# Grouping a chunked scan's 64-column matmuls by two chunks, with the steps around them moved

## The chip, the cores and the metric

The kernel runs on one core of a Trainium2 chip. The metric is the time of the whole program on the device in microseconds (us), the median of several runs. The core has a matrix engine (TensorE, PE in the profile, with PEld for its weight loads), a vector engine (VectorE, DVE), an activation engine (ScalarE, ACT), a general engine (GpSimd, POOL) and SyncE (SP), which here only issues DMAs. Each engine works through its own instructions in a fixed order and waits for the others by semaphores.

## The reference

Two layers over a sequence of 1024 positions with 1024 features: first a gated MLP that mixes positions inside chunks, then a Mamba-2 mixer. The change touches the second one only:

```python
xbc = silu(causal_depthwise_conv(xbc, conv_w, conv_b))      # x, B, C
dt  = softplus(dt_raw + dt_bias);  A = -exp(a_log)
dA_cs = cumsum(dt * A)                                      # inside each chunk of 128 positions
decay = exp(where(causal, dA_cs[l] - dA_cs[s], -inf))
w_ls  = (C @ B.T) * decay * dt                              # 128 x 128 per chunk and head
y_diag = w_ls @ x
states = (B * exp(dA_cs[-1] - dA_cs) * dt).T @ x            # per chunk
prev[c + 1] = prev[c] * exp(dA_cs[-1]) + states[c]          # over the chunks
y_off  = (C @ prev) * exp(dA_cs)
y = y_diag + y_off + x * d_skip
gated = rmsnorm(y * silu(z)) over each group of 256 features
h = h + gated @ w_out
```

There are 8 groups of 4 heads with 64 features each, a state of 128 per group, and 8 chunks of 128 positions.

## The kernel before, in words

The part in question is `scans()`. It goes through 64 steps `n`, one for each pair of group `g` and chunk `c` (chunk innermost), and writes the instructions of every engine in that order by hand (`tc.manual_schedule()`); each engine then executes its own list in order. For one chunk there are these pieces:

- `load`: a DMA brings the cumulated decays of the chunk's 4 heads to a tile `wl` (128x512; 4 such buffers). `decay`: ACT turns it into exponentials (L1582 four times, then L1584).
- `pe_a`: PE transposes x (two tiles) and B (L1576) and multiplies C by B (L1577) into one PSUM tile `tp`.
- `tokens`: DVE scales x out of `tp` (L1590) and masks the C·B product (L1592), ACT copies B (L1594), POOL scales x once more (L1595). Together they fill the tile `cw`.
- `weights`: DVE multiplies the exponentials by the masked product (L1600), so `wl` now holds w_ls.
- `pe_b`: PE's part that needs all this. Four matmuls with 64-column weights give y_diag (L1609: head pairs write to the lower and upper 64 partitions of `yy`), two give y_off from the state of the chunk before (L1613), one gives this chunk's own state (L1620, `sp`).
- `carry` (POOL, L1630) and `update` (DVE, L1639, or L1637 for the first chunk) step the state on.
- `out`: DVE multiplies y_off by its decay (L1651), adds the skip path to y_diag (L1654 twice), and POOL adds the two (L1657). `gate`: POOL multiplies by silu(z) (L1661).
- Every fourth chunk, the sums of squares for the group norm: `squares` (ACT, L1672), `sum_a` (POOL, L1679), `sum_b` (PE: matmuls with one column of ones, L1685, into the free half of `sp`; then two ACT copies of one row each, L1689), `sum_c` (a DMA). `group_rstd` reads these back and makes the reciprocal root (DVE L1704, L150 to L153).

In between, `project(upto)` emits background matmuls, six per step of its counter (L134 to L136, 128x512 each, one float32 product split in three): the input projections of later groups up to step 50, output-projection products after that. Behind each 48 of them stands an accumulator `ab` that has to pass the convolution: ACT starts it (L1311), DVE adds three taps (L1305), and after two accumulators ACT applies silu (L1416, which loads another activation table first; the next exponential loads the old table again). These conv pieces sit in a list `queue`; `drain()` emits one per chunk, and the beginning of the next accumulator emits what is still left of the older ones. Preparing the projections' weights takes a cast on ACT (L111) and a subtraction of 128x1024 on DVE or, in the scan, on POOL (L112).

For chunk n the order in the loop is: `pe_b(n)`, half of the background matmuls, `pe_a(n+2)`, `weights(n+1)`, `update(n)`, `out(n)`, `decay(n+2)`, `carry(n+1)`, `drain()`, `tokens(n+2)`, `gate(n)`, `load(n+3)`, the pieces of the norm, the other half of the background.

Of the kernel before, what the change touches and what calls it, by code (L numbers as in the profile page):

```python
# [11 lines left out]
ALU = mybir.AluOpType  # L12
# [3 lines left out]
P = 128  # L16
# [6 lines left out]
G = 8  # L23
# [6 lines left out]
def kernel(  # L30
# [21 lines left out]
    nc = tc.nc  # L52
    x = x[0]
    out = out[0]
# [19 lines left out]
    def k1(shape, name):  # L74
        return sb.tile(shape, F32, name=name, tag="k1", bufs=3)
# [21 lines left out]
    def sm(name):  # L97
        return ps[0].tile([P, 512], F32, name=name, tag="sm", bufs=n_sm[0])
# [65 lines left out]
    ones = cst.tile([P, P], F32, name="ones")  # L164
# [387 lines left out]
    for gp in range(G // 2):  # L552
# [4 lines left out]
        if gp == 1:  # L557
# [9 lines left out]
            for h in range(2):  # L567
# [9 lines left out]
                for k in range(4):  # L577
                    g = h * 4 + k
# [648 lines left out]
    V = nc.vector  # L1227
# [319 lines left out]
    class Scan:  # L1547


        def __init__(self, g, eng):  # L1550
            self.g, self.st, self.eng = g, sts[g], eng
            self.wl, self.tp, self.cw, self.ps, self.state = {}, {}, {}, {}, {}
            if g < G - 1:
                gd.append(dr.tile([P, 2, T], F32, name=f"g_d{g}"))
            else:
                gd.append(self.st["x"])
# [43 lines left out]
            V.tensor_tensor(out=wl, in0=wl, in1=self.cw[c][:, 640:768].unsqueeze(1).broadcast_to([P, 4, P]),  # L1600
                            op=ALU.mult)

        def pe_b(self, c, ends=None):

            w, wl = self.cw[c], self.wl.pop(c)
            yy = sm("yy")
            for j in range(4):
                pt, f = j // 2, j % 2
                nc.tensor.matmul(out=yy[f * 64:(f + 1) * 64, pt * P:(pt + 1) * P], lhsT=w[:, j * 64:(j + 1) * 64],  # L1609
                                 rhs=wl[:, j, :], start=True, stop=True)  # L1610
            if c > 0:
                for pt in range(2):
                    nc.tensor.matmul(out=yy[:, 256 + pt * P:384 + pt * P],  # L1613
                                     lhsT=self.state[c - 1][:, pt * P:(pt + 1) * P], rhs=self.x(3, c),
                                     start=True, stop=True)
            sp = None
            if c < 7 or ends is not None:
                sp = sm("sp")
            if c < 7:
                nc.tensor.matmul(out=sp[:, 0:256], lhsT=w[:, 512:640], rhs=w[:, 256:512], start=True, stop=True)  # L1620
            if ends is not None:
                ends.sum_b(sp[:, 256:512], 2 if ends.g == G - 1 else 1)
            self.ps[c] = yy, sp

        def carry(self, c):

# [7 lines left out]
        def update(self, c):  # L1634
            if c == 0:
                self.state[0] = k1([P, 256], "state")
                V.tensor_copy(out=self.state[0], in_=self.ps[0][1][:, 0:256])  # L1637
            elif c < 7:
                V.tensor_tensor(out=self.state[c], in0=self.ps[c][1][:, 0:256], in1=self.state[c], op=ALU.add)  # L1639

        def y(self, c):

# [1 line left out]
                return self.z(c)  # L1644
            return self.cw[c][:, 768:1024].rearrange("p (m l) -> p m l", m=2)

        def out(self, c):
            yy, t2 = self.ps.pop(c)[0], self.y(c)
            if c > 0:
                t1 = k1([P, 2, P], "t1")  # L1650
                V.tensor_tensor(out=t1, in0=yy[:, 256:512].rearrange("p (m l) -> p m l", m=2),  # L1651
                                in1=self.st["ze", c // 4][:, 2:4, c % 4 * P:c % 4 * P + P], op=ALU.mult)
            for pt in range(2):
                V.scalar_tensor_tensor(t2[:, pt, :], self.x(pt, c), dsk[:, 2 * self.g + pt:2 * self.g + pt + 1],  # L1654
                                       yy[:, pt * P:(pt + 1) * P], ALU.mult, ALU.add)
            if c > 0:
                self.eng.tensor_tensor(out=t2, in0=t2, in1=t1, op=ALU.add)  # L1657

        def gate(self, c):
# [21 lines left out]
        def sum_b(self, pr=None, n=1):  # L1681
            pr = sm("pr") if pr is None else pr
            for m in range(n):
                for h in range(2):
                    nc.tensor.matmul(out=pr[h * 64:h * 64 + 1, 0:256], lhsT=ones[:, 0:1],  # L1685
                                     rhs=self.sq[:, m, h * 256:(h + 1) * 256], start=m == 0, stop=m == n - 1)
            self.sr = self.sq[:, 1, 0:256]
            for h in range(2):
                nc.scalar.copy(out=self.sr[h * 64:h * 64 + 1], in_=pr[h * 64:h * 64 + 1, 0:256])  # L1689
# [143 lines left out]
    def scans():  # L1833


        chunks = [(g, c) for g in range(G) for c in range(8)]
        N, M = len(chunks), 50
        scan, rs, ran = {}, {}, [0]
        total = 32 * len(plain)

        def fill():
            yield from pj
            yield from bo.product(1, hook_b)

# [12 lines left out]
        def at(f, n, *a):  # L1857
            if 0 <= n < N:
                g, c = chunks[n]
                if g not in scan:  # L1860
                    scan[g] = Scan(g, nc.gpsimd)
                getattr(scan[g], f)(c, *a)

        prefetch(0, 0)
        project(AHEAD // 2 + 1)
        while todo or late:
            convolve()
        for n in range(2):
            at("load", n)
        drain(1)  # L1870
        for n in range(2):
            at("decay", n)
        drain(len(queue))
        at("pe_a", 0), at("tokens", 0), at("weights", 0)
        drain(len(queue))
        project(AHEAD)
        at("pe_a", 1), at("tokens", 1), at("weights", 1)
        at("load", 2)
        for n, (g, c) in enumerate(chunks):
            if n == M + 3:  # L1880
                drain(len(queue))
            elif n == N - 9:
                for k in range(2):
                    bo.get("a", 0, 0, k)
            elif n == N - 7:
                end["scan"] = scan[G - 1]
                bo.get("b", 0, 0, 0)
            p = g if c >= 4 else g - 1
            at("pe_b", n, scan[p] if c % 4 == 3 and p >= 0 else None)
            project(want(n + .5))  # L1890
            at("pe_a", n + 2)
            if n > 0:
                at("weights", n + 1)
            at("update", n)
            at("out", n)
            at("decay", n + 2)
            at("carry", n + 1)
            drain()
            at("tokens", n + 2)
            at("gate", n)  # L1900
            if n >= N - 7:
                k = n - N + 7
                if k % 2:
                    bo.prep(1, k // 2)
                else:
                    bo.ready(0, 0, k // 2)
            at("load", n + 3)
            th = 0 if c >= 4 else 1
            if p >= 0:
                sc = scan[p]  # L1910
                if p == G - 1:
                    if c == 5:
                        sc.gate_half(th), sc.squares(th)
                elif c % 4 == 0:
                    sc.squares(th)
                elif c % 4 == 1:
                    sc.store(th)
                    sc.sum_a()
            if c % 4 == 0 and n >= 8:
                scan[g - 1].sum_c(1 - th)  # L1920
            if g > 0:
                if c == 5:
                    rs[g] = group_rstd(g - 1, 0, T)
                elif c == 6:
                    rs[g][0]()
                elif c == 7:
                    rs[g][1]()
            if c == 0 and g > 1:
# [44 lines left out]
    with tc.manual_schedule():  # L1973
        scans()
        into_end()
# [28 lines left out]
```

## Time and profile before

| | |
|---|---|
| runs, median (lowest to highest) | 1522.73 us (1522.0 to 1526.09) |
| profiled execution: its own time, its span | 1524.54 us, 1522.8 us |
| PE busy, PEld busy | 1477.8 us (97%), 1219.0 us (80%) |
| DVE, ACT, POOL busy | 1052.6 us (69%), 784.2 us (51%), 393.3 us (26%) |
| mean granted clock of TensorE | 0.995 |
| the loop of 64 chunks: first and last diagonal part (L1609) | 1026.67 us, 1360.14 us |

In the profile's timeline a row has the start, the length, the engine, the line, the operation, the tiles (written <- read), the shape, how many instructions of that kind follow each other, and in brackets how long the engine sat idle before it and what ended that. Lengths of matmuls overlap the next one's, so PE's pace is read from one start to the next. A matmul of 128x128 or 128x256 float32 values is recorded as two instructions (x8 are four matmuls); in the lists of a program's order it is one.

### The profile page before, as it was taken

How to read it: one execution, taken by the hardware profiler on the slowest of the kernel's cores; microseconds unless marked ns; L12 is line 12 of the kernel's file. 1: busy time of each engine (PE TensorE's matmuls, PEld its weight loads, DVE VectorE, ACT ScalarE, POOL GpSimd, SP SyncE). 2: the span in 40 equal slices, each digit the busy share in tenths (PEclk: the TensorE clock that was granted, in tenths of full speed). 3: DMA queues.
4: the chain of work that ended last, by engine and by line, in shares of the span. 5: the costliest groups of instructions: out<-in, count | busy, mean ns of one | idle time of the engine just before them, and what ended most of it. 6: DMA issues, size and time to landing. Idle time of an engine off the chain costs nothing. (4 is left out here: it accounts for less than half of the span.)

```text
span 1522.8 us, 21294 instructions
## 1 busy us (share of the span) xinstructions
PE 1477.8 (97%) x7834; PEld 1219.0 (80%) x7834; DVE 1052.6 (69%) x1712; ACT 784.2 (51%) x1257; POOL 393.3 (26%) x435
## 2 busy tenths in 40 slices
PE   6899999999999999999999999999999999999997
PEld 6899988888888888877778888877777777777875
DVE  7956566676666645678646467867677677688876
ACT  6533332322332445556656566656676666756463
POOL 1111010000000023202021223207576766642221
PEclk9999999999999999999999999999999999999999
DMA  5554323332322999947277978687666665579972
GB/s 182 140 172 141 105 89 113 105 111 93 116 96 82 351 256 239 250 130 159 97 172 153 207 152 166 139 241 208 181 153 187 160 184 139 168 250 279 258 149 111
DMA packets 175976, 254.45 MB, mean 167 GB/s; under 512 B 16400, under 2 KB 103168, under 8 KB 172672
## 3 DMA queue, kind: packets, MB, share of 16 engines
q1 hardware_dynamic: 124768, 168.93, 36.2%
q0 software_dynamic: 41168, 66.07, 22.3%
q10 hardware_dynamic: 9936, 18.09, 3.3%
q8 instruction: 62, 1.02, 0.3%
q14 instruction: 42, 0.34, 0.1%
HBM read 186.14 MB, written 51.18 MB: 156 GB/s over the span
## 5 line engine op out<-in xcount | busy, mean ns | idle before, releaser
L134 PE MATMUL acc<-hh,wh 128*128 128x512 f32 x868 | 340.9, 393 | 3.0 <-ACT wh L111 2.2
L136 PE MATMUL acc<-hh,wl 128*128 128x512 f32 x868 | 339.1, 391 | 4.3 <-DVE wl L112 4.3
L135 PE MATMUL acc<-hl,wh 128*128 128x512 f32 x868 | 338.0, 389 | 0.0
L112 DVE TENSOR_TENSOR wl<-wr,wh 128x1024 fp32r<-128x1024 f32 (+1 forms) x97 | 115.5, 1193 | 127.7 <-ACT wh L111 127.6
L136 PEld LDWEIGHTS acc<-hh,wl 128*128 128x128 f32 x868 | 162.9, 188 | 42.2 <-DVE wl L112 8.4
L134 PEld LDWEIGHTS acc<-hh,wh 128*128 128x128 f32 x868 | 163.0, 188 | 39.2 <-ACT wh L111 4.3
L135 PEld LDWEIGHTS acc<-hl,wh 128*128 128x128 f32 x868 | 163.1, 188 | 32.9
L292 ACT COPY u<-acc 128x512 f32<-128x512 f32 x115 | 66.7, 582 | 193.4 <-PE acc L136 192.1
L111 ACT CAST wh<-wr 128x1024 fp32r<-128x1024 f32 (+1 forms) x113 | 116.3, 1030 | 95.4 <-PE acc L135 56.7
L136 PE MATMUL acc<-wh,hl 128*128 128x256 f32 x448 | 128.6, 287 | 4.9 <-DVE hl L403 3.5
L134 PE MATMUL acc<-wh,hh 128*128 128x256 f32 x448 | 129.0, 288 | 3.4 <-DVE wh L414 1.4
L134 PE MATMUL ab<-hh,wh 128*128 128x512 f32 x288 | 128.2, 445 | 2.1 <-DVE x L1305 1.1
L135 PE MATMUL acc<-wl,hh 128*128 128x256 f32 x448 | 128.1, 286 | 1.3 <-DVE wl L417 1.3
L136 PE MATMUL ab<-hh,wl 128*128 128x512 f32 x288 | 113.4, 394 | 0.0
L135 PE MATMUL ab<-hl,wh 128*128 128x512 f32 x288 | 112.3, 390 | 0.0
L136 PEld LDWEIGHTS acc<-wh,hl 128*128 128x128 f32 x448 | 87.2, 195 | 6.0 <-DVE hl L403 4.2
L134 PEld LDWEIGHTS acc<-wh,hh 128*128 128x128 f32 x448 | 87.1, 195 | 4.3 <-ACT hh L396 1.6
L135 PEld LDWEIGHTS acc<-wl,hh 128*128 128x128 f32 x448 | 87.2, 195 | 1.7 <-DVE wl L417 1.5
L1582 ACT ACTIVATE wl<-wl,tk 128x128 f32<-128x128 f32 x256 | 81.6, 392 | 1.3 <-DMA wl<-cs_d 1.0
L135 PE MATMUL bo<-wl,xh 128*128 128x512 f32 x192 | 76.4, 398 | 3.6 <-DVE wl L738 1.8
L645 POOL DMA_DIRECT2D y_d<-y x8 | 4.4, 548 | 290.9 <-DVE y L642 290.9
L112 DVE TENSOR_TENSOR wl<-t,wh 128x1024 fp32r<-128x1024 f32 (+1 forms) x38 | 45.4, 1196 | 48.9 <-ACT wh L111 48.7
(312 smaller groups left out, 3243.2 us busy)
## 6 DMA issues: line engine op xcount, KB each, us to landing
wr<-in_a_w_in_dram SPq DMA_DIRECT2D x48, 512.0 KB, 3.7
wl<-cs_d SPq DMA_DIRECT2D x64, 256.0 KB, 3.4
wr<-in_b_w_in_dram SPq DMA_DIRECT2D x30, 512.0 KB, 7.1
wb<-in_a_w_out_dram SPq DMA_DIRECT2D x10, 1024.0 KB, 12.2
wb<-in_b_w_out_dram SPq DMA_DIRECT2D x10, 1024.0 KB, 11.4
wr<-in_b_w_in_dram SPq DMA_DIRECT2D x36, 256.0 KB, 7.1
v<-v_d SPq DMA_DIRECT2D x8, 1024.0 KB, 4.8
y_d<-y POOLq DMA_DIRECT2D x8, 1024.0 KB, 5.8
```

The lines of the kernel that those rows point to most:

```text
L111: nc.scalar.copy(out=hi, in_=src)
L112: return (eng or nc.vector).tensor_tensor(out=lo, in0=src, in1=hi.bitcast(F32), op=ALU.subtract)
L134: nc.tensor.matmul(out=o, lhsT=l[0], rhs=r[0], start=start, stop=False, **kw)
L135: nc.tensor.matmul(out=o, lhsT=l[0], rhs=r[1], start=False, stop=False, **kw)
L136: nc.tensor.matmul(out=o, lhsT=l[1], rhs=r[0], start=False, stop=stop, **kw)
L292: nc.scalar.copy(out=self.u[n][:, i], in_=a)
L645: store = lambda: nc.gpsimd.dma_start(out=y_d[-1], in_=y)
L1582: nc.scalar.activation(wl[:, j, :], wl[:, j, :], AF.Relu, scale=-1.0, bias=tokc(2, c, self.g)[:, j:j + 1])
```

## The change

The steps of a chunk are regrouped, with nothing else computed:

- `pe_b` is split. `diagonal(c)` makes y_diag of chunks c and c+1 in one stretch of eight matmuls into the two halves of one PSUM tile `yy` (L1611), at even chunks only. `own` (L1619) and `off` (L1628) go to a tile `os`, one per chunk.
- `sum_b` uses 64 columns of ones (L1694) and a PSUM tile of its own, and stands right behind `diagonal`, a chunk later than before. Its `sum_c` follows in the same step.
- In odd chunks `pe_a(n+2)` follows `own` and `off` at once, ahead of the background.
- `weights(n+2)` now follows `tokens(n+2)` in step n, in every step. Before, `weights(n+1)` stood in step n.
- `decay` runs three chunks ahead (n+3), and two `load`s (n+4, n+5) stand behind `diagonal`.
- `out` is split: `skip` (L1657) stands behind `diagonal` for the first chunk and behind `drain` for the second; `out` (L1664, L1666) is at the end.
- The last group's first half is gated and squared one chunk earlier (c = 4).

```diff
+        def diagonal(self, c):
+            yy = sm("yy")
+            for e in range(2):
+                w, wl = self.cw[c + e], self.wl.pop(c + e)
+                self.yy[c + e] = yy[:, e * 256:(e + 1) * 256]
+                for j in range(4):
+                    pt, f = j // 2, j % 2
+                    nc.tensor.matmul(out=self.yy[c + e][f * 64:(f + 1) * 64, pt * P:(pt + 1) * P],
+                                     lhsT=w[:, j * 64:(j + 1) * 64], rhs=wl[:, j, :], start=True, stop=True)
...
-                    nc.tensor.matmul(out=pr[h * 64:h * 64 + 1, 0:256], lhsT=ones[:, 0:1],
+                    nc.tensor.matmul(out=pr[h * 64:h * 64 + 64, 0:256], lhsT=ones[:, 0:64],
...
-        at("load", 2)
+        at("load", 2), at("load", 3)
+        at("decay", 2)
...
-            at("pe_b", n, scan[p] if c % 4 == 3 and p >= 0 else None)
-            project(want(n + .5))
-            at("pe_a", n + 2)
-            if n > 0:
-                at("weights", n + 1)
-            at("update", n)
+            if c % 2 == 0:
+                at("diagonal", n)
+                if c % 4 == 0 and g > 0:
+                    scan[g - 1].sum_b()
+                elif n == N - 2:
+                    scan[g].sum_b(n=2)
+                at("own", n), at("off", n)
+                at("load", n + 4), at("load", n + 5)
+                at("skip", n)
+                project(want(n + .5))
+                at("pe_a", n + 2)
+                if c % 4 == 0 and g > 0:
+                    scan[g - 1].sum_c(1 if c else 0)
+                at("update", n)
+                at("decay", n + 3)
+                at("carry", n + 1)
+                drain()
+                at("skip", n + 1)
+            else:
+                at("own", n), at("off", n)
+                at("pe_a", n + 2)
+                at("update", n)
+                project(want(n + .5))
+                at("decay", n + 3)
+                at("carry", n + 1)
+                drain()
+            at("tokens", n + 2)
+            at("weights", n + 2)
             at("out", n)
-            at("decay", n + 2)
-            at("carry", n + 1)
-            drain()
-            at("tokens", n + 2)
             at("gate", n)
...
-            at("load", n + 3)
...
-                    if c == 5:
+                    if c == 4:
                         sc.gate_half(th), sc.squares(th)
...
-            if c % 4 == 0 and n >= 8:
-                scan[g - 1].sum_c(1 - th)
```

How it moves instructions is seen best at two places. The first is PE at a sum of squares, before (step 7: the 64-column diagonal part, y_off, the sums, and the first background matmul):

```order
L136 MATMUL ab<-hh,wl 128x512
L1609 MATMUL yy<-wl,cw 64x128 x4
L1613 MATMUL yy<-xbc,state 128x128 x2
L1685 MATMUL sp<-gsq,ones 1x256 x2
L134 MATMUL ab<-hh,wh 128x512
```

After the change the same sums stand in step 8:

```order
L136 MATMUL ab<-hh,wl 128x512
L1611 MATMUL yy<-wl,cw 64x128 x8
L1694 MATMUL pr<-gsq,ones 64x256 x2
L1619 MATMUL os<-cw 128x256
L134 MATMUL ab<-hh,wh 128x512
```

One stretch of 64-column matmuls stands where two stretches of diagonals and one of sums stood.

The second place is DVE around the weights of chunks 12 and 13, the first and the last L1600 shown. Before:

```order
L1600 TENSOR_TENSOR wl<-wl,cw 128x512
L1639 TENSOR_TENSOR state<-sp,state 128x256
L1651 TENSOR_TENSOR t_8975<-yy,ze 128x256
L1654 SCALAR_TENSOR_TENSOR cw<-xbc,dsk,yy 128x128 x2
L1305 SCALAR_TENSOR_TENSOR x<-ab,par,x 128x1023
L1590 TENSOR_TENSOR cw<-tp,tk 128x256
L1592 TENSOR_TENSOR cw<-tp,mask 128x128
L1600 TENSOR_TENSOR wl<-wl,cw 128x512
```

After:

```order
L1600 TENSOR_TENSOR wl<-wl,cw 128x512
L1664 TENSOR_TENSOR t_8941<-os,ze 128x256
L1646 TENSOR_TENSOR state<-os,state 128x256
L1305 SCALAR_TENSOR_TENSOR x<-ab,par,x 128x1023
L1590 TENSOR_TENSOR cw<-tp,tk 128x256
L1592 TENSOR_TENSOR cw<-tp,mask 128x128
L1600 TENSOR_TENSOR wl<-wl,cw 128x512
```

The convolution's first tap (L1305) stands ahead of chunk 13's weights in both. Before, the last row belonged to step 12 and PE asked for it in step 13; now it belongs to step 11 and PE asks for it in step 12, behind chunk 12's diagonal part.

On ACT, the same place (the silu of step 11 and the exponentials behind it), before:

```order
L111 CAST wh<-wr 128x1024
L1416 ACT_TABLE_LOAD
L1416 ACTIVATE bc<-bc 128x2048
L1311 ACTIVATE x<-ab,par 128x1024
L1582 ACTIVATE wl<-wl,tk 128x128 x4
L1584 ACT_TABLE_LOAD
L1584 ACTIVATE wl<-wl 128x512
```

After:

```order
L1582 ACTIVATE wl<-wl,tk 128x128 x4
L1584 ACTIVATE wl<-wl 128x512
L1594 COPY cw<-tp 128x128
L111 CAST wh<-wr 128x1024
L1416 ACT_TABLE_LOAD
L1416 ACTIVATE bc<-bc 128x2048
L1311 ACTIVATE x<-ab,par 128x1024
```

Chunk 13's exponentials (L1582, L1584) have moved ahead of the silu, to the step before. The convolution's start (L1311), for which the tap on DVE waits, still stands behind the silu.

More of the change, by code (lines that the diff above doesn't have):

```diff
@@ L1551, in __init__ @@
             self.g, self.st, self.eng = g, sts[g], eng
-            self.wl, self.tp, self.cw, self.ps, self.state = {}, {}, {}, {}, {}
+            self.wl, self.tp, self.cw, self.yy, self.os, self.state = {}, {}, {}, {}, {}, {}
             if g < G - 1:
@@ L1601, in weights, with own, off @@
                             op=ALU.mult)
-        def pe_b(self, c, ends=None):
-            w, wl = self.cw[c], self.wl.pop(c)
+        def diagonal(self, c):
             yy = sm("yy")
[L1607 to L1610, printed above, removed]
+            for e in range(2):
[5 more added lines that the diff above has]
+                                     lhsT=w[:, j * 64:(j + 1) * 64], rhs=wl[:, j, :], start=True, stop=True)
+        def own(self, c):
+            w = self.cw[c]
+            if c < 7:
+                self.os[c] = sm("os")
+                nc.tensor.matmul(out=self.os[c][:, 0:256], lhsT=w[:, 512:640], rhs=w[:, 256:512],
+                                 start=True, stop=True)
+        def off(self, c):
+            if c == 7:
+                self.os[c] = sm("os")
             if c > 0:
                 for pt in range(2):
-                    nc.tensor.matmul(out=yy[:, 256 + pt * P:384 + pt * P],
+                    nc.tensor.matmul(out=self.os[c][:, 256 + pt * P:384 + pt * P],
                                      lhsT=self.state[c - 1][:, pt * P:(pt + 1) * P], rhs=self.x(3, c),
                                      start=True, stop=True)
[L1616 to L1623, printed above, removed]
         def carry(self, c):
@@ L1636, in update @@
                 self.state[0] = k1([P, 256], "state")
-                V.tensor_copy(out=self.state[0], in_=self.ps[0][1][:, 0:256])
+                V.tensor_copy(out=self.state[0], in_=self.os[0][:, 0:256])
             elif c < 7:
-                V.tensor_tensor(out=self.state[c], in0=self.ps[c][1][:, 0:256], in1=self.state[c], op=ALU.add)
+                V.tensor_tensor(out=self.state[c], in0=self.os[c][:, 0:256], in1=self.state[c], op=ALU.add)
         def y(self, c):
@@ L1645, in y, with skip @@
             return self.cw[c][:, 768:1024].rearrange("p (m l) -> p m l", m=2)
[L1647 to L1652, printed above, removed]
+        def skip(self, c):
+            yy, t2 = self.yy.pop(c), self.y(c)
             for pt in range(2):
@@ L1655, in out @@
                                        yy[:, pt * P:(pt + 1) * P], ALU.mult, ALU.add)
+        def out(self, c):
+            os, t2 = self.os.pop(c), self.y(c)
             if c > 0:
+                t1 = k1([P, 2, P], "t1")
+                V.tensor_tensor(out=t1, in0=os[:, 256:512].rearrange("p (m l) -> p m l", m=2),
+                                in1=self.st["ze", c // 4][:, 2:4, c % 4 * P:c % 4 * P + P], op=ALU.mult)
                 self.eng.tensor_tensor(out=t2, in0=t2, in1=t1, op=ALU.add)
```

## The prediction

> **What bounds the kernel now.** I read first the busy times by stage, cut at the first and last parts of the scan. Columns: stretch, its length, then for PE, PEld, DVE, ACT and POOL the busy time (and instructions), the granted clock, the DMA share.
>
> ```profile
> 1026.67:1325.47 298.80, 296.77 (x1806) 226.75 (x1807) 216.07 (x453) 203.04 (x423) 208.41 (x231) 1.00 0.62 172
> 1325.47:1384.28 58.81, 56.00 (x315) 41.42 (x314) 50.70 (x94) 40.39 (x70) 19.62 (x23) 1.00 0.77 263
> 1384.84:1388.25 3.41, 3.41 (x10) 2.64 (x9) 3.41 (x6) 3.10 (x4) 0.14 (x1) 0.50 0.87 149
> ```
>
> For the first 298.80 us of the scan PE is busy 296.77: whatever takes PE less time shortens it, whatever makes PE wait lengthens it. DVE has 216.07 of 298.80, ACT 203.04, so both can be late for a moment without being the bound. In the second row DVE has 50.70 of 58.81 and PE 56.00. The third row is for later.
>
> Next, PE's timeline, where the starts give its pace:
>
> ```profile
> 1057.18 0.39 PE L136 MATMUL ab<-hh,wl 128*128 128x512 f32 x1
> 1057.50 0.66 PE L1609 MATMUL yy<-wl,cw 128*64 128x128 f32 x8
> 1058.09 0.71 PE L1613 MATMUL yy<-xbc,state 128*128 128x128 f32 x4
> 1058.63 0.60 PE L1620 MATMUL sp<-cw 128*128 128x256 f32 x2
> ...
> 1063.08 0.71 PE L1613 MATMUL yy<-xbc,state 128*128 128x128 f32 x4
> 1063.72 0.60 PE L1685 MATMUL sp<-gsq,ones 128*1 128x256 f32 x4
> 1064.25 0.50 PE L134 MATMUL ab<-hh,wh 128*128 128x512 f32 x1
> 1064.58 0.39 PE L135 MATMUL ab<-hl,wh 128*128 128x512 f32 x1
> 1064.81 0.40 PE L136 MATMUL ab<-hh,wl 128*128 128x512 f32 x1
> ...
> 1065.74 0.49 PE L1576 MATMUL tp<-ident,xbc 128*128 128x128 f32 x3
> 1066.06 0.39 PE L1577 MATMUL tp<-xbc 128*128 128x128 f32 x2
> 1066.21 0.47 PE L134 MATMUL ab<-hh,wh 128*128 128x512 f32 x1
> ```
>
> Background matmuls follow each other at 0.23 us (1064.58 to 1064.81). The first 64-column matmul comes 0.32 after the last of them (1057.18 to 1057.50), 0.09 late. Its stretch lasts 0.59 (to 1058.09), the four full-width instructions behind it 0.54 (to 1058.63), though 128 columns cost 0.107 (three transposes in 0.32, 1065.74 to 1066.06), so four should take 0.43: 0.11 too much. What the stretch itself should take, the doubled sums of the last step tell:
>
> ```profile
> 1361.37 1.03 PE L1685 MATMUL sp<-gsq,ones 128*1 128x256 f32 x8
> ```
>
> Eight instructions of 256 columns last 1.03, four lasted 0.60 (row 1063.72). So four more cost 0.43, and eight of 128 columns also 0.43, where 0.59 is taken: 0.16 too much. A change of the weights' width and back thus costs 0.09 + 0.16 + 0.11 = 0.36 us. The sums are the same case: 0.64 instead of 0.54 ahead of them (1063.08 to 1063.72), 0.53 instead of 0.43 for them, 0.33 instead of 0.23 behind (1064.25 to 1064.58): 0.30 us.
>
> **The gains.** Diagonals in pairs save 32 of 64 such changes: 32 x 0.36 = 11.5 us. Sums inside a stretch cost their 0.43 and nothing else; 15 of 16 move there (the last stands alone behind the loop): 15 x 0.30 = 4.5 us. More columns of ones should change no matmul's length while its moving side stays at 256: the diagonals' 64 weight columns and the transposes' 128 both came to 0.107 for 128 moving columns. Two kinds of waits should go:
>
> ```profile
> PEld ab L134 <- DVE x L1305: 1.5, 2, 0.9
> ...
> PEld sp L1685 <- POOL gsq L1679: 0.9, 1, 0.9
> ```
>
> PE waited twice, 1.5 us, for the last tap to free an accumulator, in the second half of an even step; the tap now stands in that step's first 3.5 us and PE asks at about 4. The sums waited 0.9 us for POOL's addition, done at chunk 1 or 5, and now stand three chunks behind it instead of two. Together 2.4 (0 if both come back). Gains: 18.4 us.
>
> **The losses.** `diagonal(n)` needs the weights of chunk n+1 one step sooner than `pe_b(n+1)` did. PE executes in order, so behind a missing weight wait the own state, y_off, the background and the next transposes. Where the weights come late is read from DVE and ACT:
>
> ```profile
> 1066.49 0.42 DVE L1590 TENSOR_TENSOR cw<-tp,tk 128x256 f32<-128x256 f32 x1 [1.73 <-PE tp L1577]
> ...
> 1201.36 0.41 DVE L1590 TENSOR_TENSOR cw<-tp,tk 128x256 f32<-128x256 f32 x1
> ...
> 1208.57 1.28 DVE L1305 SCALAR_TENSOR_TENSOR bc<-ab,par,bc 128x1023 f32<-128x1023 f32 x1 [2.39 <-ACT bc L1311]
> 1209.77 0.41 DVE L1590 TENSOR_TENSOR cw<-tp,tk 128x256 f32<-128x256 f32 x1
> ...
> 1211.68 1.70 DVE L1600 TENSOR_TENSOR wl<-wl,cw 128x512 f32<-128x512 f32 x1 [1.30 <-ACT wl L1584]
> ```
>
> ```profile
> 1202.06 0.27 ACT L1594 COPY cw<-tp 128x128 f32<-128x128 f32 x1 [2.69 <-DVE cw L1592]
> 1202.22 1.06 ACT L1672 ACTIVATE gsq<-ze 128x1024 f32<-128x1024 f32 x1
> 1203.18 1.03 ACT L111 CAST wh<-wr 128x1024 fp32r<-128x1024 f32 x1
> 1204.23 1.28 ACT L1416 ACT_TABLE_LOAD   x1
> ```
>
> ```profile
> L1600 DVE TENSOR_TENSOR wl<-wl,cw x64: 679/951/2418, 1025.7 to 1359.4; 128x512 f32<-128x512 f32 x64
> ```
>
> **Start.**
>
> ```profile
> 1027.73 2.42 DVE L1600 TENSOR_TENSOR wl<-wl,cw 128x512 f32<-128x512 f32 x1 [0.44 <-ACT cw L1594]
> ```
>
> Chunk 1's weights ended at 1027.73 + 2.42 = 1030.15. Nothing ahead of them changes. PE ended chunk 0's diagonals here:
>
> ```profile
> 1027.25 0.70 PE L1620 MATMUL sp<-cw 128*128 128x256 f32 x2
> ```
>
> It now needs chunk 1's at once and stands from 1027.2 to 1030.2: 3.0 us (1.5 if the multiplication took its median 0.951 instead of 2.42).
>
> **A silu in an odd step.** The row 1204.23 is the table load ahead of a silu. Behind it in ACT's order comes the convolution's start; the tap on DVE waits for that until 1208.57 (4.34 later), tokens start at 1209.77 (1.20 later), weights at 1211.68, of which 1.30 was a wait for exponentials. That wait goes, since they are a step earlier now. So weights start 0.61 after tokens, take 0.95, and PE may start 0.1 later: 4.34 + 1.20 + 0.61 + 0.95 + 0.1 = 7.2 us behind the table load. Nothing shortens this chain, since tap, tokens and weights keep their order on DVE. When does the load start? Tokens start 0.75 behind the transposes (1065.74 to 1066.49); an even step ends 1.9 behind its transposes (0.47 for them, to 1066.21, and six background matmuls), so they start 1.1 before the odd step. ACT's copy follows 0.70 later (1201.36 to 1202.06), cast and load 1.2 behind it, or 2.2 with the squares between (to 1204.23). So the load starts 0.8 into the odd step, or 1.8 with squares. PE reaches the second chunk's diagonals 4.8 into it: own state 0.43, y_off 0.43, transposes 0.47, twelve background matmuls with a late first one 2.9, the first chunk's diagonals 0.5. The order of the changed program has four odd steps of this kind. Step 11: 0.8 + 7.2 - 4.8 = 3.2. Step 25: squares, but six more background matmuls in the step before: 1.8 - 1.4 + 7.2 - 4.8 = 2.8. Step 33: squares and six more in the step itself: 1.8 + 7.2 - 6.2 = 2.8. Step 47, a last chunk without own state: 0.8 + 7.2 - 4.4 = 3.6. Together 12.4; 8 if each load starts 1.1 sooner, 16 if PE's background is as much shorter.
>
> **A silu in an even step** leaves DVE one chunk more. From the tap on it has 1.20 + 0.5 (skip) + 1.6 (tokens, weights) + 0.7 (decay of y_off, update) + 1.2 (tap) + 1.6, 6.8 us, and 1.2 ahead of it for the rest of the load's chain; PE needs some 10 us for both steps. Three such steps: 1.3 us, nearly all in step 18 (0 to 4).
>
> **The other pairs.** In an odd step transposes start 0.87 in, tokens 0.75 later, weights end 1.66 after that, 3.3 us in; with an update and a tap in front of them about 4.0, against 4.8. So 0.8 us is left, which a POOL subtraction beside the multiplication can use up (0.951 became 1.70 in the row 1211.68). I take 1 us for all of them (0 to 8).
>
> **The end.** In the stretch from 1325.47 on, DVE is nearly full, so three pairs and two sums save nothing: 3 x 0.36 + 2 x 0.30 = 1.7 (0 to 3).
>
> **At nothing**: DVE, ACT and POOL issue the same number of instructions; the same loads go out on SP, two at a time behind `diagonal`, over a step ahead of the exponentials that read them. If that cover went, ACT would wait and the case would be the last rival but one. The last group's earlier gating only moves 1.2 us of DVE.
>
> Losses: 3.0 + 12.4 + 1.3 + 1.0 + 1.7 = 19.4, gains 18.4: 1.0 us slower.
>
> **The clock.** Five standstills of about 3 us are new in the scan. In the profile PE stood once like that, shorter:
>
> ```profile
> 1384.28 0.50 PE L135 MATMUL bo<-wl,xh 128*128 128x512 f32 x1 [1.81 <-DVE wl L738]
> 1384.61 0.42 PE L136 MATMUL bo<-wh,xl 128*128 128x512 f32 x1
> 1384.84 0.61 PE L134 MATMUL bo<-wh,xh 128*128 128x512 f32 x1
> 1385.25 0.63 PE L135 MATMUL bo<-wl,xh 128*128 128x512 f32 x1
> ```
>
> After an idle 1.81 us the next matmuls follow at 0.41 instead of 0.23, and the window from 1384.84 to 1388.25 has a granted clock of 0.50 for 3.41 us. At some 0.42 each, 8 matmuls fit where 14.8 did: 6.7 x 0.23 = 1.5 us lost. Part of such a window may fall into the standstill itself, and an unlucky split over two windows may not trigger: 5 x 0.9 x 1.35 = 6.1 us (0 to 8.5).
>
> [...]
>
> **Sum.** 1.0 + 6.1 = 7.1 us over the profiled execution's 1524.54, 1531.6. That execution lay 1.8 over the median of the runs, 1522.73; on the median the forecast is 1530.
>
> **Rivals.**
> 1. The clock holds in all but the longest standstill: 1.0 + 1.5 gives 1525. For it: shorter idle times in the scan left the clock at 1.00 (first row). Against it: the row 1384.28.
> 2. The other side: the silu chains are hidden. If ACT came to the load 2.4 us or more sooner in each odd step, the four would cost some 0.5 each, with no clock loss: -18.4 + 3.0 + 2.0 + 1.3 + 1.0 + 1.7 = -9.4, 1513. It decides once the four and the clock together cost under 6.8 us (18.4 - 3.0 - 1.3 - 1.0 - 1.7 - 4.6). For it: before, these chains hardly touched PE. Against it: they then had a whole step of about 5 us more.
> 3. The 0.8 us of ordinary pairs isn't there, and 8 us more are lost: 1538. For it: 216 of 299 us on DVE, in bursts.
> 4. The change doesn't save what it says, because the extra belongs to each 64-column matmul: 11.5 less, 1541. Against it: 1.03 against 0.60.
>
> **Chances.** Forecast 0.41 (its own range 1526 to 1536), rivals 0.24, 0.24, 0.07 and 0.04. The range 1510 to 1538 takes in rival 2 for the most part and leaves out about 0.1 on each side. About 0.3% (4.6 us) is what a measurement can tell from no change: faster 0.24 (rival 2), same 0.28 (rival 1 and the low end of the forecast), slower 0.48.
>
> **What would show it.** Right: 32 diagonal stretches of some 1.02 us; sums of 0.43 with no gap; PE idle about 3 us inside the first stretch and inside those of chunks 12, 26, 34 and 48, released by L1600; windows of half clock behind them. Wrong: waits there under 1 us, a tap that doesn't wait for ACT, clock 1.00 all through the scan, or waits of PE at other pairs.

## The result and the profile after

The changed kernel took 1537.5 us (median of 4 runs, 1534.42 to 1540.98) against 1524.11 (4 runs, 1522.0 to 1526.09): a ratio of 1.0089, 95% interval 1.0076 to 1.0103. It is 13.4 us slower. The profiled execution took 1537.53 us, span 1535.8: 13.0 more than the one before, and the sums below are made on this pair.

The busy times by stage of the changed kernel, cut at the same work as before (from the first diagonals to those of chunk 56, then to the idle time in front of L738's product), and three windows of half clock; columns as in the prediction:

```profile
1026.72:1337.39 310.67, 291.07 (x1803) 236.83 (x1803) 219.53 (x452) 204.66 (x427) 199.06 (x228) 0.97 0.59 165
1337.39:1398.25 60.86, 56.09 (x318) 43.98 (x318) 52.98 (x94) 38.77 (x66) 23.42 (x26) 0.97 0.80 257
1029.02:1035.85 6.83, 5.64 (x22) 4.45 (x22) 2.69 (x6) 3.26 (x7) 2.22 (x3) 0.50 0.49 142
1172.38:1179.21 6.83, 5.15 (x20) 4.19 (x21) 4.40 (x11) 3.75 (x8) 3.91 (x5) 0.50 0.70 193
1298.68:1302.09 3.41, 3.41 (x11) 2.63 (x10) 3.12 (x7) 2.47 (x7) 1.16 (x2) 0.50 0.39 138
```

The first stage went from 298.80 to 310.67 us, 11.9 of the 13.0. PE is busy 291.07 there instead of 296.77, so it has less to do, although half-clock stretches make part of that work longer (at 1032.71 and 1033.14 two background matmuls start 0.43 us apart, at full clock 0.23); it waits 19.6 us instead of 2.0. The granted clock is 0.97 instead of 1.00.

PE's timeline shows both sides. First the regular pairs; then the diagonals that waited, one row for the second half of each pair (idle time and its releaser in brackets):

```profile
1051.13 1.09 PE L1611 MATMUL yy<-wl,cw 128*64 128x128 f32 x16
1052.16 0.70 PE L1619 MATMUL os<-cw 128*128 128x256 f32 x2
...
1062.10 1.09 PE L1611 MATMUL yy<-wl,cw 128*64 128x128 f32 x16
...
1071.25 1.09 PE L1611 MATMUL yy<-wl,cw 128*64 128x128 f32 x16
1072.18 0.60 PE L1694 MATMUL pr<-gsq,ones 128*64 128x256 f32 x4
1072.71 0.70 PE L1619 MATMUL os<-cw 128*128 128x256 f32 x2
...
1082.21 1.09 PE L1611 MATMUL yy<-wl,cw 128*64 128x128 f32 x16
```

```profile
1030.21 1.12 PE L1611 MATMUL yy<-wl,cw 128*64 128x128 f32 x8 [2.83 <-DVE wl L1600]
...
1095.70 0.66 PE L1611 MATMUL yy<-wl,cw 128*64 128x128 f32 x8 [3.23 <-DVE wl L1600]
...
1174.06 1.12 PE L1611 MATMUL yy<-wl,cw 128*64 128x128 f32 x8 [3.54 <-issue]
...
1222.00 0.66 PE L1611 MATMUL yy<-wl,cw 128*64 128x128 f32 x8 [2.73 <-issue]
...
1297.32 0.66 PE L1611 MATMUL yy<-wl,cw 128*64 128x128 f32 x8 [3.53 <-DVE wl L1600]
...
1308.54 0.66 PE L1611 MATMUL yy<-wl,cw 128*64 128x128 f32 x8 [1.19 <-DVE wl L1600]
```

An undisturbed stretch of two chunks takes 1.03 us to the next instruction (1051.13 to 1052.16). The first five rows of the second fence are standstills of 2.83, 3.23, 3.54, 2.73 and 3.53 us: the start, and chunks 12/13, 26/27, 34/35 and 48/49. The last, chunk 51, is the longest of the others. Where the releaser reads "issue", the rows of DVE around chunk 27 below show the weights ending 0.1 us ahead of PE; at chunk 35 they ended at 1221.90, also 0.1 us ahead.

### The profile page after: what moved, and what is told of

It reads as the page before. It is cut to its first block, busy times and chain, and to the rows that moved or that the text cites. A ratio compares the mean times of both kernels' runs of the same rounds, so it can differ in the third digit from the quotient of the medians.

```text
span 1535.8 us, 21276 instructions
## 1 busy us (share of the span) xinstructions
PE 1472.8 (96%) x7834; PEld 1233.2 (80%) x7834; DVE 1058.5 (69%) x1712; ACT 784.3 (51%) x1257; POOL 387.7 (25%) x435
## 5 line engine op out<-in xcount | busy, mean ns | idle before, releaser
L135 PE MATMUL acc<-hl,wh 128*128 128x512 f32 x868 | 338.4, 390 | 0.0
L112 DVE TENSOR_TENSOR wl<-wr,wh 128x1024 fp32r<-128x1024 f32 (+1 forms) x97 | 115.6, 1193 | 127.7 <-ACT wh L111 127.6
L135 PEld LDWEIGHTS acc<-hl,wh 128*128 128x128 f32 x868 | 163.1, 188 | 32.7
L135 PE MATMUL acc<-wl,hh 128*128 128x256 f32 x448 | 129.3, 289 | 1.1 <-DVE wl L417 1.1
L134 PE MATMUL ab<-hh,wh 128*128 128x512 f32 x288 | 123.6, 429 | 1.3 <-DVE zt L995 0.7
L135 PE MATMUL ab<-hl,wh 128*128 128x512 f32 x288 | 113.8, 395 | 0.0
L135 PEld LDWEIGHTS acc<-wl,hh 128*128 128x128 f32 x448 | 88.4, 197 | 1.8 <-DVE wl L417 1.4
L1582 ACT ACTIVATE wl<-wl,tk 128x128 f32<-128x128 f32 x256 | 81.6, 391 | 8.0 <-DMA wl<-cs_d 7.7
L135 PE MATMUL bo<-wl,xh 128*128 128x512 f32 x192 | 75.9, 395 | 4.9 <-DVE wl L112 2.4
L112 DVE TENSOR_TENSOR wl<-t,wh 128x1024 fp32r<-128x1024 f32 (+1 forms) x38 | 45.4, 1196 | 49.5 <-ACT wh L111 49.5
## 6 DMA issues: line engine op xcount, KB each, us to landing
wb<-in_a_w_out_dram SPq DMA_DIRECT2D x10, 1024.0 KB, 11.3
```

Of the source, the lines that this page charges most:

```text
L112: return (eng or nc.vector).tensor_tensor(out=lo, in0=src, in1=hi.bitcast(F32), op=ALU.subtract)
L134: nc.tensor.matmul(out=o, lhsT=l[0], rhs=r[0], start=start, stop=False, **kw)
L135: nc.tensor.matmul(out=o, lhsT=l[0], rhs=r[1], start=False, stop=False, **kw)
L1582: nc.scalar.activation(wl[:, j, :], wl[:, j, :], AF.Relu, scale=-1.0, bias=tokc(2, c, self.g)[:, j:j + 1])
```

## Experiments

The first theory was that of the prediction: the tap waits for ACT's silu and stands ahead of the weights on DVE, PE waits idle for it, and the clock halves behind that. All times are medians; "the changed kernel" is the one above. The kernel before, run beside each group, had medians of 1523.3 to 1523.4.

### Useless matmuls in the waits

```diff
+                for _ in range(12 if e and 8 * self.g + c in (0, 12, 26, 34, 48) else 0):
+                    nc.tensor.matmul(out=yy[:, 256:512], lhsT=ident, rhs=self.cw[c][:, 0:256], ...)
                 for j in range(4):
```

> Twelve useless matmuls of 256 columns (2.6 us of PE) stand between the two halves of the diagonals of chunks 0/1, 12/13, 26/27, 34/35 and 48/49 of the changed kernel; the result isn't changed, since the second half overwrites them. Theory (a standstill of PE of about 3 us is followed by half clock, and that is lost time on top of the wait): PE works through 2.6 of each wait of 2.7 to 3.5 us, the weights are no later than before, the three half-clock windows of the scan (6.83, 6.83 and 3.41 us) do not come, and the time falls by 5 to 7 us from 1537.5 to about 1531. Rival (the half clock costs nothing because PE would have waited for DVE and ACT anyway, or it isn't the standstill that brings it): no change or, with 13 us more work on PE, up to 3 us slower.

Measured: 1541.22 us, 3.7 more, with runs that overlap (1538.18 to 1541.72 against 1534.42 to 1540.98). The size was wrong: a matmul of 256 columns is recorded as two rows, and twelve took 5.45 us, not 2.6. In the rows below, 24 of them with 128 columns of weights take 5.38 us to the next start, 0.22 each. In the changed kernel's single records the two rows of a sum's matmul (L1694, 64 columns of weights) start 0.007 us apart, and the next matmul 0.21 behind the second.

```profile
1028.24 0.66 PE L1613 MATMUL yy<-wl,cw 128*64 128x128 f32 x8
1028.83 5.45 PE L1610 MATMUL yy<-cw,ident 128*128 128x256 f32 x24
1034.21 0.66 PE L1613 MATMUL yy<-wl,cw 128*64 128x128 f32 x8
```

Five such fills are 27.2 us. If they replaced the waits alone (15.9 us), 11.3 more was due; this profiled execution was 4.2 longer than the changed kernel's. So some 7 us went with the waits. Behind the fills of chunks 1 and 27 the background matmuls followed at 0.24 and 0.23 us (1035.56 to 1035.80, 1181.12 to 1181.35), not at 0.43, and the mean clock of the whole execution was 0.994, the changed kernel's 0.989. (In the trace five other waits for weights are left, 3.2 us.) Again with six:

> As the run with twelve useless matmuls, but six: a matmul of 256 columns, recorded as two rows, took 0.45 us there and not the 0.215 that the first expectation counted, so six fill 2.7 us of the five waits (2.83, 3.23, 3.54, 2.73, 3.53). Theory (the half clock behind a standstill is lost time): no half clock in the scan, and 5 to 7 us less than the changed kernel, about 1531. Rival (the half clock falls into time that PE waits anyway): within 2 us of 1537.5.

Measured: 1531.17 us, 6.3 less, clock 1.00 over the 305.5 us from the first diagonals to those of chunk 56. Thirty matmuls more, none of them useful, made the kernel faster: the half clock behind the waits is lost time by itself. In the profiled pair 5.1 us of the gain lie in that stretch (310.67 to 305.5); another 1.6 lie behind it, where the changed kernel had a half-clock stretch at 1356.70 and this run had none (the mean clock of the whole execution is 0.996 against 0.989, an estimated 20 us less of half clock, and the four stretches from 1029.02 to 1360.12 had 20.5). So the two runs put the price of the half clock in the scan at 5 to 7 us of the 13.

### The tap behind the weights

```diff
                 at("carry", n + 1)
-                drain()
             at("tokens", n + 2)
             at("weights", n + 2)
+            if c % 2:
+                drain()
```

> In odd steps of the changed kernel the convolution's piece (tap on DVE, now and then its start on ACT) is issued behind tokens and weights instead of ahead of them; ACT's order at the silus stays as it is. Theory (the four long waits come from the tap that waits for ACT's silu and stands ahead of the weights on DVE): the waits at chunks 12/13, 26/27, 34/35 and 48/49 (3.2, 3.5, 2.7, 3.5 us) and the half clock behind two of them go, 17 us together, and the time is about 1520; the wait at the start stays. Rival 1 (the weights are late because of ACT's exponentials or of DVE's sheer load): the waits stay, the time is 1535 to 1540. Rival 2 (the later tap frees its accumulator later, and PE waits for that instead): 1525 to 1535 with idle time at L134 released by L1305.

Measured: 1519.87 us, 17.6 less than the changed kernel, and a ratio of 0.9977 (0.9965 to 0.9990) to the kernel before. What PE waited for in the scan, first in the changed kernel, then here (us in total, times, longest):

```profile
PE yy L1611 <- DVE wl L1600: 13.0, 9, 3.5
PE yy L1611 <- issue: 6.3, 2, 3.5
```

```profile
PE yy L1611 <- DVE wl L1600: 2.5, 2, 2.3
PE ab L134 <- DVE bc L1305: 1.9, 1, 1.9
```

ACT's order at the silus is the same in both; DVE's is not. The diagonals' waits fell from 13.0 + 6.3 to 2.5 us, nearly all of it the start. Rival 2 is there as well, but small: 1.9 us at one accumulator, with a half-clock window behind it (clock 0.99 from 1026.67 to 1340 us), and 1.0 at another. The own state also waited 1.5 us for DVE's L1664 (twice) and 1.5 us for POOL's subtraction.

### The convolution's start ahead of the silu

```diff
             if queue:
-                queue[-1] += ops.pop(0)
+                queue[-1] = ops.pop(0) + queue[-1]
```

> The changed kernel with the next accumulator's convolution start on ACT ahead of the silu instead of behind it; DVE's order stays, the tap still ahead of the weights. Theory (the tap waits for a start that stands behind the silu's table load and its 2048 columns on ACT): the chain is shorter by the table load and the silu, about 3 us, the four waits at chunks 12/13, 26/27, 34/35 and 48/49 shrink from 2.7 to 3.5 us to under 0.7, and 15 us or more are gone, 1520 to 1523; part of it comes back where the exponentials behind the silu are 1 us later. Rival (the tap is late for another reason, such as the accumulator itself or DVE's load): waits of 2 us or more stay, 1532 or more.

Measured: 1519.8 us, 17.7 less. Here DVE's order is the changed kernel's and only ACT's differs. What PE waited for at the diagonals (to be set against the changed kernel's 13.0 + 6.3 above):

```profile
PE yy L1611 <- DVE wl L1600: 7.4, 7, 2.4
```

The start's 2.4 us are in it. The four waits shrank to 0.64, 0.65, 1.11 and 1.91 us: the first two as expected, the other two not so far, and behind the last stands a half-clock window (1294.91 to 1298.32). Either end of the chain, cut alone, takes most of the loss away; that settles its path.

### Chunk 1's diagonals later

```diff
-                at("diagonal", n)
+                at("diagonal", n, (0, 1) if n else (0,))
...
                 project(want(n + .5))
+                if n == 0:
+                    at("diagonal", n, (1,))
```

> Only chunk 1's diagonals of the changed kernel are moved: behind the first half of step 0's background instead of straight behind chunk 0's. Theory (2.83 us of wait and 6.83 us of half clock come from the wait for chunk 1's weights alone): the first pair's 14.81 us become about 9.5, the time falls by 5 us to 1532. Rival (PE's lead is given back at the next place where it waits, the tap of step 11): under 2 us are left of it.

Measured: 1533.84 us, 3.7 less where 5 were due; its runs (1531.7 to 1538.75) overlap with the changed kernel's, so a gain is not shown. The second half now waited for DVE's L1657, which reads the first half of the same PSUM tile. In its profiled execution, the slowest of the four, the mean clock was 0.988, the changed kernel's 0.989, and the first stage was no shorter (311.2 us against 310.7):

```profile
1031.23 0.66 PE L1611 MATMUL yy<-wl,cw 128*64 128x128 f32 x8 [1.19 <-DVE cw L1657]
```

### Single chunks' diagonals, three attempts

Each has the changed kernel's order with the pairs undone; the second gives each chunk its own PSUM tile and one load a step, the third moves that load to the step's end. Main lines of the third's edit:

```diff
-            for e in range(2):
+            for e in range(1):
...
+            at("diagonal", n)
             if c % 2 == 0:
-                at("diagonal", n)
...
-                at("load", n + 4), at("load", n + 5)
...
+            at("load", n + 4)
             project(want(n + 1))
```

> The changed kernel with each chunk's diagonals in its own step again (64 stretches instead of 32), all else as changed: sums beside diagonals, weights a step early, decays three chunks ahead. Theory (only the pairing makes the weights' lateness visible): no wait over 1 us at the diagonals, no half clock in the scan, the 23 us of the five places gone and 11.5 us of width changes back: 1537.5 - 23 - 1.5 + 11.5 = about 1524, and 3 to 5 us under the kernel before if the sums bring 4.5. Rival (the other order of weights, decays and taps is itself the loss): still 1530 or more, with waits of PE that the kernel before didn't have.

> Each chunk's diagonals in its own step and its own PSUM tile, with one load of decays per step behind them instead of two behind the even one (in the first attempt the second load stood up to 7.9 us at the head of SP's queue, and the next group's inputs behind it came late); sums, weights a step early, decays three ahead as in the changed kernel. Theory (only the pairing makes the weights' lateness visible): no wait over 1 us at the diagonals, no half clock in the scan, 1537.5 - 23 - 1.5 + 11.5 = about 1524, 2 or 3 less if the sums keep their 4.5. Rival (the new order of weights, decays and taps is a loss by itself): 1530 or more.

> Each chunk's diagonals in its own step, as before, with the load of decays four chunks ahead now at the end of a step, behind the next group's inputs on SP's queue. (With the load ahead of them, those inputs waited at the queue's head for the diagonals to free a decay buffer, and the transposes of 7 steps were 0.7 to 3.6 us late.) Theory (only the pairing makes the weights' lateness visible): no wait over 1 us at the diagonals or transposes, 1520 to 1526. Rival (the new order of weights, decays and taps is a loss by itself): 1530 or more.

Measured: 1543.62, 1547.56 and 1545.21 us, all slower than the changed kernel. One half of the theory held: in none of the three did PE wait over 0.25 us at the diagonals in the scan. The time went elsewhere. In the first, the largest waits are those of the transposes for their inputs (11.9 us in six waits; 15.2 in seven in the second run), and SP's queue says why. Its waits in the first run, then in the changed kernel, then PE's row for the transposes of chunk 24 in the first run:

```profile
SPq L1571 <- PE yy L1611: 176.5, 44, 7.9
```

```profile
SPq L1571 <- PE yy L1611: 95.4, 36, 4.7
SPq L1571 <- DVE wl L1600: 71.6, 22, 5.8
```

```profile
1159.55 0.52 PE L1576 MATMUL tp<-ident,xbc 128*128 128x128 f32 x3 [3.42 <-DMA xbc<-xbc_d]
```

A load waits for its decay buffer, which PE frees only at the diagonals; with pairs that comes a step sooner for every second chunk. The prefetch of the next group's inputs is queued behind it, and PE waits for these. In total SP waits about as long in the changed kernel, but never 7.9 us at a time, and there PE has no wait of this kind. With the load behind the prefetch most of it goes (2.5 us left), and another wait is larger (own state of chunk 12):

```profile
1094.54 1.19 PE L1619 MATMUL os<-cw 128*128 128x256 f32 x2 [6.46 <-DVE t L1664]
```

L1664 of step 11 stands on DVE behind tap, tokens and weights, and holds a bank that the own state waits for. So a late tap can cost without pairs too, by way of the banks; but it is one of the four silus in one of the three runs, and there ACT itself began late: it had waited 7.45 us (to 1083.81) for a load of decays. The rival's 1530 or more came true, by waits for loads and banks. What the new order would cost unpaired with the silu's chain cut wasn't tried, nor the pairing alone in the old order.

### The sums alone

The kernel before, with 64 columns of ones, right behind the next chunk's diagonals; in the second run with a PSUM tile of their own:

```diff
-                    nc.tensor.matmul(out=pr[h * 64:h * 64 + 1, 0:256], lhsT=ones[:, 0:1],
+                    nc.tensor.matmul(out=pr[h * 64:h * 64 + 64, 0:256], lhsT=ones[:, 0:64],
...
-            at("pe_b", n, scan[p] if c % 4 == 3 and p >= 0 else None)
+            at("pe_b", n, scan[g - 1] if c % 4 == 0 and g > 0 else scan[g] if n == N - 1 else None)
```

> The kernel before with the sums of squares alone changed: 64 columns of ones, right behind the diagonals of the next chunk. Theory (the width changes cost 0.30 us per sum, and 0.9 us of waiting for POOL's addition goes): 15 x 0.30 + 0.9 = 5.4 us less, ratio 0.9965. Rival (PE's time there is hidden by or given back to other waits, or 64 columns of sums cost more than one): ratio 0.999 to 1.002.

> As the first run with the sums alone, but with a PSUM tile for each sum. (There the own state's matmul wrote the other half of the sums' tile and waited 0.7 to 4.2 us, twelve times, for ACT to copy the sums out.) Theory (0.30 us of width changes per sum, and 0.9 us of waiting for POOL): 15 x 0.30 + 0.9 = 5.4 us less than the kernel before, ratio 0.9965. Rival (given back to other waits, such as a late free bank among the four): ratio 0.999 to 1.003.

Measured: 1544.04 us, ratio 1.0139 (1.0119 to 1.0159), and 1523.68 us, 0.9996 (0.9986 to 1.0005). Waits of PE, first and second run:

```profile
PE sp L1620 <- ACT gsq L1687: 18.6, 13, 4.2
```

```profile
PE tp L1576 <- DMA xbc<-xbc_d: 2.6, 1, 2.6
PE bo L135 <- DVE wl L112: 1.4, 2, 0.7
PE ab L134 <- DVE x L1305: 1.0, 2, 0.7
PE tp L1576 <- DVE state L1638: 0.6, 1, 0.6
```

In the first, the own state wrote the other half of the sums' tile and waited 18.6 us for ACT's copies out of it; the changed kernel has that tile apart. In the second, each move of a sum shortened the scan by 0.28 to 0.30 us, as costed, but one late input (2.6 us) and waits at the end took part of it back: 2.7 us were left in the profiled execution (span 1520.1), and nothing that the timing can tell.

### Two and three remedies together

> Two remedies of the changed kernel together: the convolution's start ahead of the silu on ACT (alone 1519.8), and chunk 1's diagonals behind the first half of step 0's background, now in a PSUM tile of their own (in the first attempt they shared chunk 0's tile and waited 1.19 us for DVE to read it). Theory: the start's 2.39 us and the half clock behind it go too, 3.5 to 4.5 us: 1515.5 to 1516.5, ratio 0.9955. Rival (the start's gain is given back at the next late weights, those of chunk 13): 1519, ratio 0.997.

> The two remedies together (1517.8), and the convolution's piece of an odd step behind tokens and weights as well, except where five pieces are left in the queue: there it is an accumulator's last tap or a start, and a later last tap held PE for 1.88 us at chunk 39 in the run that moved the taps of all odd steps. Theory (what is left of late weights is the tap's 1.2 us ahead of them): the waits of 0.64, 0.65, 1.11 and 1.92 us at the second chunks of pairs and the half clock behind the last go, about 4 us: 1513 to 1515, ratio 0.994. Rival (the weights there are late for POOL's subtraction beside them, or the later taps hold PE at the accumulators): 1517 to 1519, ratio 0.996 to 0.998.

The first is the start ahead of the silu and chunk 1's diagonals later, in a tile of their own; the second adds, in odd steps:

```diff
-                drain()
+                after_weights = len(queue) < 5
+                if not after_weights:
+                    drain()
             at("tokens", n + 2)
             at("weights", n + 2)
+            if c % 2 and after_weights:
+                drain()
```

Measured: 1517.79 us, ratio 0.9967 (0.9955 to 0.9979), and 1511.51 us, 0.9914 (0.9897 to 0.9930). The first fell between its two expectations: PE still waited 0.91 us for chunk 1, and late weights kept 6.2 us in seven waits. The second beats the kernel before by 11.9 us and the changed one by 26, more than expected; which of its waits gave the surplus was not isolated. What PE waited for in it up to 1340 us:

```profile
PE tp L1576 <- DVE state L1644: 1.9, 1, 1.9
...
PE ab L134 <- DVE x L1305: 1.0, 1, 1.0
PE tp L1576 <- ACT cw L1594: 0.7, 1, 0.7
PE yy L1611 <- DVE wl L1600: 0.6, 2, 0.3
PE yy L1611 <- issue: 0.6, 1, 0.6
```

No wait at the diagonals is over 0.6 us there any more, although this profiled execution was the slowest of its five (1517.43 us).

## Why the prediction was right, and where it was off

It said slower, 1530, range 1510 to 1538; measured 1537.5, inside the range and at its edge. The increase was 13.4 us where 7.3 were forecast.

**Width changes.** Right. In the starts above, chunks 4 and 5 take 10.97 us (1051.13 to 1062.10). The kernel before:

```profile
1046.15 0.66 PE L1609 MATMUL yy<-wl,cw 128*64 128x128 f32 x8
...
1067.77 0.66 PE L1609 MATMUL yy<-wl,cw 128*64 128x128 f32 x8
...
1078.66 0.66 PE L1609 MATMUL yy<-wl,cw 128*64 128x128 f32 x8
```

There it was 11.35 (1046.15 to 1057.50, shown earlier), so 0.38 was saved where 0.36 was costed. Chunks 6 and 7 lost a sum as well: 9.15 instead of 10.27, 1.12 for 0.36 + 0.30 + the sum's 0.43. Chunks 8 and 9 got it: 10.96 against 10.89, +0.07 for 0.43 - 0.36. That more columns of ones cost nothing also held: a sum's four rows take 0.53 us to the next start before (1063.72 to 1064.25) and after (1072.18 to 1072.71). But the reason given, 0.107 us for 64 and for 128 columns of weights alike, set a matmul of two rows against a transpose of one. By the useless matmuls above (0.45 us each, against 0.22 from one of a sum's to the next) full width would have cost about twice as much: an estimate.

**The chain behind a silu in an odd step.** Right, to 0.1 us. ACT, then DVE, in the changed kernel at chunk 27, the first half of whose pair stood at 1169.86:

```profile
1166.78 1.28 ACT L1416 ACT_TABLE_LOAD   x1
1168.07 1.92 ACT L1416 ACTIVATE bc<-bc 128x2048 f32<-128x2048 f32 x1
1169.89 1.18 ACT L1311 ACTIVATE x<-ab,par 128x1024 f32<-128x1024 f32 x1
```

```profile
1171.11 1.28 DVE L1305 SCALAR_TENSOR_TENSOR x<-ab,par,x 128x1023 f32<-128x1023 f32 x1 [3.96 <-ACT x L1311]
1172.31 0.41 DVE L1590 TENSOR_TENSOR cw<-tp,tk 128x256 f32<-128x256 f32 x1
1172.64 0.28 DVE L1592 TENSOR_TENSOR cw<-tp,mask 128x128 f32<-128x128 f32 x1
1172.95 1.00 DVE L1600 TENSOR_TENSOR wl<-wl,cw 128x512 f32<-128x512 f32 x1
```

From the table load to the tap 4.33 us (4.34 predicted), 1.20 to tokens, 0.64 to weights (0.61), 1.00 for them (0.95), 0.11 to PE: 7.28 against 7.2. The five standstills were predicted as 3.0, 3.2, 2.8, 2.8 and 3.6, together 15.4; they are 15.9. Only chunk 27's, 3.54 us instead of 2.8, is off by more than 0.2: ACT's load began 1.2 us into its step (1165.58 to 1166.78), not 0.4.

**The clock.** Right in kind; 6.1 us predicted. The five places lengthened the scan by 23.0 us in all (their pairs' periods against before, less what an undisturbed pair gained), 7.1 more than their waits, and the fills give the same size. But it was three events and not five small ones: behind the start and chunk 27 the half clock lasted 6.83 us, behind chunk 49 3.41, and behind chunks 13 and 35 there was none. The run with chunk 1's diagonals later, which stood 1.19 us at the start instead of 2.83, had no less half clock (mean clock 0.988 against 0.989). So the total came out close partly by luck. The factors 0.9 and 1.35 of the 6.1 us were the author's estimates; no run shows them, only the three events that took some 7 us together.

**Ordinary pairs and silus in even steps.** The step that failed by size: 2.3 us predicted, some 4.8 measured, at eight other pairs (by their periods against before, as above). The largest is 1.7 at chunks 50/51, where the last row of PE's waits shows 1.19. The "0.8 us left" for an odd step's weights was too much: in pairs 2/3, 4/5, 10/11, 18/19 and 42/43, which did not wait, the weights ended only 0.4 us ahead of PE. A multiplication beside POOL's subtraction (1.98 us at chunk 15, 1.97 at 29, 1.32 at 51; the median of all 64 is 0.952) uses that up, and that came three times in the scan; what made the others late was not followed up.

**Removed waits and the end.** Of 2.4 us about 1.7 went, POOL's and one of the two for a tap. The last stage was costed at no gain (it has four pairs, not the three that were counted, which is 0.4 us); from chunk 56 to the end of the program it lost 1.1 us (13.0 - 11.9), with a half-clock stretch from 1356.70 to 1360.12 in the place of the one at 1384.84 before.

These small terms make up the difference: 2.5 (other pairs) + 1.1 (the end) + 1.0 (clock) + 0.7 (waits that stayed) + 0.5 (the five standstills) = 5.8 of 13.0 - 7.1 = 5.9 us. Each was inside its own range, and all of them erred to the same side. They are read from one pair of traces; no run isolates them.

**Loads at nothing.** Held: ACT waited three times for decays, 4.2 us at most, and PE's periods there are the undisturbed ones. But in the first experiments with single chunks the same loads blocked SP's queue: the cover was not independent of the pairs.

## What to carry to other kernels

A step that is moved ahead must be checked on each engine that feeds it, behind the rarest work in its queue: here some 17 us came from four silus, which the averages (DVE 216 of 299 us) don't show. Where the chain was late, it was cheaper to reorder one instruction on DVE or ACT than to give up the new grouping. Short standstills of PE had a second price in the clock: here even useless matmuls in their place made the kernel 6.3 us faster. That background work would do at least as well there was not tried.

## What the hardware showed that was not expected

The half clock did not begin where a standstill ended. In the changed kernel's scan it began at 1029.02, 1.64 us into the 2.83 of the start; at 1172.38, 1.86 us into the 3.54 of chunk 27; at 1298.68, 1.36 us behind the end of chunk 49's 3.53; and at 1356.70, 0.32 us behind the end of a wait of 1.49 us (L135, released at 1356.38 by DVE's L112). The last three of these starts lie 143.36, 269.66 and 327.68 us behind the first: in this trace 42, 79 and 96 times 3.413 us, and the two shorter stretches lasted about that long (1298.68 to 1302.09, 1356.70 to 1360.12). (Idle times are from PE's rows, whose ends are modelled.)

In this trace the length of a standstill alone did not tell whether the clock fell. The 3.23 us at chunk 13 and the 2.73 at chunk 35 were followed by full clock (1.00 from 1088 to 1099 us and from 1219 to 1230), the wait of 1.49 us by half clock. What decided between them these rows don't show.
